# The last four gate groups of a hybrid layer as a seven-product block

## The chip, the cores and the metric

One core of a Trainium2 chip runs the whole layer. The metric is the device time of one execution in microseconds (us). Engines: PE (TensorE, matmul), DVE (VectorE), ACT (ScalarE), POOL (GpSimd), SP (SyncE, which issues most DMA transfers from a queue worked off in order). ACT issues a few transfers from its own queue.

## The reference, cut to what matters

```python
h = rms_norm(x, norm_mix_g)
y_m, y_d, y_c = ...            # mLSTM, differential attention, memory cross-attention
g_m, g_d, g_c = jnp.split(jax.nn.sigmoid(h @ w_gate + b_gate), 3, axis=-1)
merged = g_m * (y_m @ w_proj_m) + g_d * (y_d @ w_proj_d) + g_c * (y_c @ w_proj_c)
x = x + merged @ w_out
h2 = rms_norm(x, norm_mlp_g)
x = x + jnp.square(jax.nn.relu(h2 @ w_up)) @ w_down
```

There are 1024 positions and 1024 channels; `w_gate` is 1024 x 3072. Everything is float32.

## The kernel before

**Products.** A float32 product is made of three matmuls in the `fp32r` type: each operand is split into a high part (a cast on ACT) and a low part (a subtraction on DVE), by `split` (L106), and `mm3` (L117) issues high x high, high x low, low x high. The normed input stands transposed in SBUF as `hT` (8 row tiles of 128 channels, high and low, 64 KB a partition).

**Gates.** The 3072 gate columns are 12 groups of 256. `gate_steps` (L447) is a generator: a group has four quarters (two halves of 128 columns by two halves of 512 positions), a quarter 8 steps of three matmuls, 96 matmuls of 512 columns in a group. Behind a quarter ACT makes the tanh (L471) and SP stores it to DRAM (`gdr`, L472). `gate_load` (L432) loads and splits the weights of the next group, two 128-row tiles a load. The products go to two PSUM banks in turn (`mm_tile`, L144, `kmm = 2`).

**Order.** Groups 0 and 1 fill the cross-attention, 2 and 3 the mLSTM (`branch_m`). Groups 4 and 5 run by themselves. Then `branch_d` (L966), the differential attention: `d_gemm` (L859) makes q, k, v of one head after the other in steps of three matmuls, and the attention's scores, transposes and value products stand between the steps in an order written out by hand; `fill(n)` takes n steps. It begins with `fill(60)` (L1083). After each four row tiles `prep` (L865) turns q and k: a transpose on PE (`pr`), behind a power on POOL (`rsqrt_mean`, L124) and a scaling of k on DVE (`s_`, L884). Behind the last head, groups 6 to 8 are the steps. Groups 9 to 11 run by themselves after the attention. The instructions that are not pinned are placed by the framework's scheduler, on SP too, where a transfer waits in its turn.

**Buffers.** Pools are stacked: each starts at the byte of a partition where the one before it ends, and space of a closed pool is taken over by the next. `hT` lies at 3,072 to 68,608, the split weights (`wpg`, 13 tiles of 3 KB) and the raw weights (`rpg`, 3 of 3 KB) behind it to 117,760. From there come the attention's pools, or, after it, the two gate tiles. A tile of the new owner waits until the old ones at its bytes are read.

**Tail.** `tail` (L1297) starts when `hT` is closed, at byte 3,072. It multiplies the three branches' outputs (`yd` in DRAM) by their projections, first the cross-attention's. `k_tiles` (L1263) loads eight tiles of 128 x 1024 into two buffers (`yrp`, 4 KB each) and splits them into nine places of 8 KB (`ys8` first). `load_w` (L130) loads the weights into two buffers (`rp2`, 4 KB each), 512 KB for four row tiles. Its first group (`group`, L1274, `outer`) goes row tile by row tile through four banks, 12 matmuls for each. The pools ahead of `yrp` are `tone` 4,608 bytes, `ssq` 4 KB, `gl` 4 KB, `mtp` 32 KB, `mlp` 32 KB, `op` 8 KB, `hole` 7 KB and the nine `ys` of 8 KB.

**Seven products.** The MLP (`wino`, L1174) and its second half multiply 256 x 256 blocks of weights by blocks of two row tiles and two halves of the positions with seven products instead of eight. `PROD` (L1121) lists, for each, the weight block and the operand block; the blocks beyond the four plain ones are sums, made by `wino_s` on POOL (L1142) for the weights and `wino_t` on DVE and POOL (L1123) for the operand.

Of the kernel before, what the change touches and what calls it, by code (L numbers as in the profile page):

```python
# [71 lines left out]
class Layer:  # L72
# [359 lines left out]
    def gate_load(self, pool=None):  # L432

        pool = pool or self.gwp
        n = self.gate_n
        if n == 12 * NK:
            return
        g, k = divmod(n, NK)
        if k % 2 == 0:
            self.graw = self.grp.tile([P, 512], F32, tag="raw", name=self.name("raw"))  # L440
            self.nc.sync.dma_start(self.graw.rearrange("p (k n) -> p k n", k=2), self.a["wgate"][g][:, k : k + 2, :])
        t = pool.tile([P, 2, 256], F32R, tag="w", name=self.name("w"))
        self.split(t[:, 0], t[:, 1], self.graw[:, k % 2 * 256 : k % 2 * 256 + 256])
        self.gw.append((t[:, 0], t[:, 1]))
        self.gate_n = n + 1

    def gate_steps(self, runs):  # L447
# [4 lines left out]
        for run in runs:  # L452
            for r in range(run):
# [3 lines left out]
                for q in range(4):  # L457
# [505 lines left out]
                late.pop(0)[1]()  # L963
            yield True

    def branch_d(self, pool):  # L966
        nc = self.nc
        V = nc.vector
        self.pinned = True
# [5 lines left out]
        def fill(n):  # L975
            for _ in range(n):
                r = next(gemm, None)
                if r is None:
                    next(gates, None)
# [100 lines left out]
                nc.scalar.activation(y, pt, AF.Copy, scale=self.gsub)  # L1080
                self.store_y(1, hh // 2, hh % 2, y)

        fill(60)  # L1083
        for s in range(NS + 4):
            hh, i = divmod(s - 2, 4)
            if s < NS:
# [23 lines left out]
                combine(s)  # L1110
        fill(8)
        norm(15, 2)
        assert self.gdone <= 288
        while self.gdone < 288:
            next(gates)
        self.pinned = False


# [497 lines left out]
    def run(self):  # L1616
        tc, nc = self.tc, self.nc
        with ExitStack() as ctx:
# [19 lines left out]
            self.x1d = dt("x1_d", (8, P, D))  # L1638
            self.h2d = dt("h2_d", (8, P, D))
            self.rd = dt("r_d", (16, P, 7, 512))  # L1640
            with ExitStack() as c1:
                E1 = lambda *x, **k: c1.enter_context(tc.tile_pool(*x, **k))
                self.pmm = E1(name="pmm", bufs=1, space=PSUM)
# [4 lines left out]
                with ExitStack() as c2:  # L1648
# [4 lines left out]
                    with tc.tile_pool(name="ptmp", bufs=1) as tmp0, tc.tile_pool(name="ptmp2", bufs=2) as tmp, tc.tile_pool(name="ptmp8", bufs=8) as tmp8:  # L1653
# [24 lines left out]
                    self.branch_m(T3(), gm, 1, gnext)  # L1678
                with tc.tile_pool(name="wpg", bufs=13, reuse_waits="tile") as self.wp, tc.tile_pool(name="rpg", bufs=3, reuse_waits="tile") as self.rp:
                    self.gwp, self.grp = self.wp, self.rp  # L1680
                    with tc.tile_pool(name="pg", bufs=2) as self.gpool:
                        for _ in range(2 * 32):
                            next(self.gates)
                    cg.close()
                    with tc.tile_pool(name="pd", bufs=2) as pd, tc.tile_pool(name="pd3", bufs=3) as pd3, tc.tile_pool(name="pdm", bufs=1) as pdm, tc.tile_pool(name="pd5", bufs=7) as pd5, tc.tile_pool(name="pdv", bufs=5) as pdv, tc.tile_pool(name="pdv2", bufs=17) as pdv2, tc.tile_pool(name="pd4", bufs=4) as pd4:
                        self.tmask = pdm.tile([P, D], F32, name="tmask")
                        nc.gpsimd.memset(self.tmask, 0.0)
                        nc.gpsimd.affine_select(
                            out=self.tmask[:, D - P : D], in_=self.tmask[:, D - P : D], pattern=[[-1, P]],
                            compare_op=ALU.is_ge, fill=NEG, base=0, channel_multiplier=1,  # L1690
                        )
                        class T4:
                            def tile(_, shape, dt, tag, name):
                                tag = "dscr2" if tag == "gt" else tag
                                p = pd5 if tag == "draw" else pdv if tag == "drr" else pdv2 if tag == "dv" else pd4 if tag in ("dk", "dkl") else pdm if tag == "dpe1" else pd3 if tag in ("daT", "dst") else pdm if tag in ("dscr", "dscr2", "y", "dsg") else pd
                                return p.tile(shape, dt, tag=tag, name=name)
                        self.gpool = T4()
                        self.branch_d(T4())
                    with tc.tile_pool(name="pgh", bufs=2) as self.gpool:
                        for _ in self.gates:  # L1700
                            pass
            self.tail()


# [3 lines left out]
def pack(i):  # L1708
# [3 lines left out]
    def grp(w, cols):  # L1712
        return np.ascontiguousarray(w[:, cols].reshape(-1, P, len(cols)).transpose(1, 0, 2))
# [20 lines left out]
        return q.transpose(3, 2, 1, 0, 4)  # L1734

    wg = i["w_gate"][0]
    w["wgate"] = np.stack([grp(wg, r(256 * g, 256)) for g in range(12)])
# [33 lines left out]
```

## Time and profile before

| | |
|---|---|
| median of 3 runs (lowest, highest) | 2207.4 us (2206.66, 2209.99) |
| the profiled execution | 2207.4 us, of it span 2205.3 us |
| PE busy | 2162.5 us, 98% |
| DVE, ACT, POOL busy | 62%, 45%, 24% |
| matmuls of the gates (512 columns) | 1152 |

The span is the time from the first to the last instruction in the trace. Busy times of a group are unions, since matmuls overlap: their mean length is more than the distance at which they follow each other. "L91" is the matmul call that all products share, so products are told apart by their tiles: `mm<-hT,w` are products with `hT` as the moving operand (gates, mLSTM), `mm<-w,hT` the attention's rows, `sc` scores, `po` values, `tp` and `pr` transposes, `mm<-kt,w` the tail's first projection.

### The profile page before, as it was taken

How to read it: one execution, taken by the hardware profiler on the slowest of the kernel's cores; microseconds unless marked ns; L12 is line 12 of the kernel's file. 1: busy time of each engine (PE TensorE's matmuls, PEld its weight loads, DVE VectorE, ACT ScalarE, POOL GpSimd, SP SyncE). 2: the span in 40 equal slices, each digit the busy share in tenths (PEclk: the TensorE clock that was granted, in tenths of full speed). 3: DMA queues.
4: the chain of work that ended last, by engine and by line, in shares of the span. 5: the costliest groups of instructions: out<-in, count | busy, mean ns of one | idle time of the engine just before them, and what ended most of it. 6: DMA issues, size and time to landing. Idle time of an engine off the chain costs nothing.

```text
span 2205.3 us, 30616 instructions
## 1 busy us (share of the span) xinstructions
PE 2162.5 (98%) x11097; PEld 1862.0 (84%) x11097; DVE 1360.7 (62%) x2598; ACT 982.2 (45%) x1962; POOL 525.2 (24%) x696
## 2 busy tenths in 40 slices
PE   7999999999999999999999999999999999999999
PEld 5878888898899999999888888887787888788887
DVE  6643565565237777777641242544588877767779
ACT  6543354454336666666542120314444444543332
POOL 2100000000011111111000002102657655555553
PEclk9999999999999999999999999999999999999999
DMA  7123122121333333333343443436435444854444
GB/s 250 31 78 117 52 92 73 43 81 44 108 109 91 89 87 88 89 90 82 101 153 114 133 161 107 144 103 207 157 106 197 158 150 146 321 195 154 145 140 167
DMA packets 127948, 273.06 MB, mean 124 GB/s; under 512 B 12945, under 2 KB 21430, under 8 KB 125750
## 3 DMA queue, kind: packets, MB, share of 16 engines
q1 hardware_dynamic: 125494, 258.53, 37.2%
q10 hardware_dynamic: 2304, 12.58, 1.4%
q8 instruction: 87, 1.43, 0.3%
q14 instruction: 63, 0.52, 0.1%
HBM read 178.76 MB, written 67.14 MB: 112 GB/s over the span
## 4 chain that ended last, share of the span: by engine, by line
PE 86%; DVE 5%; DMA 4%; ACT 2%; issue 2%; POOL 1%; SPq 0%; DVEq 0%; ACTq 0%; POOLq 0%
PE mm L91 51%; PE p L91 22%; PE sc L91 6%; PE po L91 3%; PE tp L94 3%; DVE acc L67 1%; PE pr L94 1%; DVE wo L67 1%; DVE u L67 0%; DVE w L112 0%; DMA kraw<-y 0%; PE tp L91 0%; DMA wraw<-in_wdown 0%; DVE xts L67 0%; DMA xr<-h_d 0%
## 5 line engine op out<-in xcount | busy, mean ns | idle before, releaser
L91 PE MATMUL mm<-w,hT 128*128 128x384 f32 (+3 forms) x2496 | 471.7, 331 | 2.5 <-ACT w L111 2.4
L91 PE MATMUL mm<-hT,w 128*128 128x512 f32 x1920 | 465.6, 395 | 0.0
L91 PEld LDWEIGHTS mm<-hT,w 128*128 128x128 f32 x1920 | 353.6, 188 | 74.0
L91 PEld LDWEIGHTS mm<-w,hT 128*128 128x128 f32 x2496 | 389.0, 189 | 13.8 <-ACT w L111 3.2
L91 PE MATMUL p<-xo,wo 128*128 128x512 f32 x1344 | 311.0, 393 | 6.4 <-DVE st L1418 3.2
L91 PE MATMUL p<-xd,wo 128*128 128x512 f32 x1344 | 309.5, 392 | 5.5 <-DVE c L67 2.2
L91 PEld LDWEIGHTS p<-xo,wo 128*128 128x128 f32 x1344 | 253.0, 189 | 63.1 <-DVE u L67 3.7
L91 PEld LDWEIGHTS p<-xd,wo 128*128 128x128 f32 x1344 | 253.4, 189 | 61.4 <-DVE c L67 3.3
L91 PE MATMUL mm<-kt,w 128*128 128x512 f32 x1152 | 261.9, 389 | 0.9 <-DVE w L112 0.5
L112 DVE TENSOR_TENSOR w<-raw,w 128x256 fp32r<-128x256 f32 (+3 forms) x304 | 172.8, 588 | 138.2 <-ACT w L111 137.1
L91 PEld LDWEIGHTS mm<-kt,w 128*128 128x128 f32 x1152 | 216.1, 188 | 46.6 <-DVE w L112 1.0
L111 ACT CAST w<-raw 128x256 fp32r<-128x256 f32 (+3 forms) x304 | 154.4, 530 | 176.6 <-PE mm L91 132.1
L104 ACT CAST wo<-wraw 128x896 fp32r<-128x896 f32 x122 | 115.0, 944 | 213.6 <-PE p L91 101.7
L67 DVE TENSOR_TENSOR wo<-wraw,wo 128x896 fp32r<-128x896 f32 x122 | 143.3, 1192 | 58.5 <-ACT wo L104 58.5
L1145 POOL TENSOR_TENSOR wraw<-wraw 128x128 f32<-128x128 f32 x128 | 93.7, 732 | 253.1 <-DMA wraw<-in_wdown 122.9
L1007 ACT ACTIVATE dpe<-sc,dst,drr 128x256 f32<-128x256 f32 (+7 forms) x128 | 106.7, 833 | 95.5 <-DVE dst L1003 92.1
L999 DVE CUSTOM_DVE_ANT_0 sc<-sc,tmask 128x256 f32<-128x256 f32 (+7 forms) x128 | 97.0, 757 | 14.7 <-PE sc L91 14.1
L127 POOL TENSOR_SCALAR hss<-hss 128x4 f32<-128x4 f32 x8 | 3.3, 408 | 415.1 <-ACT mscr L752 273.0
L91 PE MATMUL sc<-dk,dq 128*128 128x512 f32 (+3 forms) x384 | 91.7, 347 | 0.0
L1148 POOL TENSOR_TENSOR wraw<-wraw 128x128 f32<-128x128 f32 x128 | 87.2, 681 | 9.9
L1146 POOL TENSOR_TENSOR wraw<-wraw 128x128 f32<-128x128 f32 x128 | 87.7, 685 | 0.0
L1147 POOL TENSOR_TENSOR wraw<-wraw 128x128 f32<-128x128 f32 x128 | 85.2, 665 | 0.0
(283 smaller groups left out, 2830.7 us busy)
## 6 DMA issues: line engine op xcount, KB each, us to landing
dk<-dsg SPq DMA_DIRECT2D x64, 256.0 KB, 4.2
wraw<-in_wup SPq DMA_DIRECT2D x64, 256.0 KB, 3.4
r_d<-xts SPq DMA_DIRECT2D x16, 1024.0 KB, 4.1
wraw<-in_wdown SPq DMA_DIRECT2D x64, 256.0 KB, 3.1
xd<-r_d SPq DMA_DIRECT2D x19, 768.0 KB, 7.3
xd<-r_d SPq DMA_DIRECT2D x14, 1024.0 KB, 6.7
raw<-in_wgate SPq DMA_DIRECT2D x48, 256.0 KB, 2.9
gates<-gt SPq DMA_DIRECT2D x48, 256.0 KB, 2.0
```

The costliest lines, as they stand in the source:

```text
L67: return self.tc.keep_in_program_order(f(*a, **k))
L91: self.pin(self.nc.tensor.matmul(out, l, r, start=start, stop=stop))
L94: self.pin(self.nc.tensor.transpose(out, x, self.ident))
L104: self.A.copy(hi, src)
L111: nc.scalar.copy(hi, src)
L112: nc.vector.tensor_sub(lo, src, f32(hi))
L999: V.tensor_tensor_reduce(out=sc[:, 0:n], in0=sc[:, 0:n], in1=self.tmask[:, D - n : D], scale=1.0, scalar=-3.0e38, op0=ALU.add, op1=ALU.max ...
L1007: nc.scalar.activation(pe[c][:, 0:n], sc[:, 0:n], AF.Exp, bias=t8[:, 2 + c : 3 + c], scale=rr[:, i, c : c + 1], accum_out=t8[:, 4 + c : 5 ...
L1145: G.tensor_add(r[:, 4], r[:, 0], r[:, 3])
L1146: G.tensor_sub(r[:, 5], r[:, 4], r[:, 1])
L1147: G.tensor_sub(r[:, 6], r[:, 1], r[:, 0])
L1148: G.tensor_sub(r[:, 7], r[:, 2], r[:, 5])
```

## The change

- Gates are direct for groups 0 to 7 only: 0 to 3 as before, group 4 by itself, 5 to 7 in the attention. The stores of groups 5 to 7 are issued by ACT.
- Groups 8 to 11 become `wino_gates`, after the attention: four runs of seven products, each four pairs of row tiles deep, in the two PSUM banks. The three plain operand blocks come from `hT`; the four summed ones (X4, X5, X6, X3; 2 MB each, 16 KB a partition) are loaded from DRAM (`hcd`). The weights come in quads; POOL makes four sums of 256 columns for each of eight loads, and 56 tiles of 256 columns are split.
- `h_sums` makes the four summed blocks and stores them: per pair of row tiles two additions, three subtractions on DVE and one on POOL, then four splits and stores of 512 KB. It advances at every third step of group 4 and at every fourth of `fill(60)`.
- The pools of the attention are reordered and wait by tile; group 4's tanh goes into one tile instead of two. The pools of `wino_gates` stand from byte 117,760: gate tiles 4 KB, `fev` 16 KB, three raw rings of 8 KB, then X3, X6, X5, X4.

```diff
@@ gate_load
-        if n == 12 * NK:
+        if n == 8 * NK:
@@ gate_steps
-                    nc.sync.dma_start(self.gdr[ft, :, s], t)
+                    (nc.scalar if g > 4 else nc.sync).dma_start(self.gdr[ft, :, s], t)
@@ branch_d
-        fill(60)
+        for n in range(60):
+            fill(1)
+            if n % 4 == 3:
+                next(sums, None)
...
-        assert self.gdone <= 288
-        while self.gdone < 288:
+        assert self.gdone <= 256
+        while self.gdone < 256:
             next(gates)
+    def h_sums(self, pool):
+        nc, V, G = self.nc, self.nc.vector, self.nc.gpsimd
+        for kp in range(4):
+            b = []
+            for k in range(2):
+                t = pool.tile([P, D], F32, tag="dpe0", name=self.name("hb"))
+                V.tensor_add(t, f32(self.hT[:, 2 * kp + k, 0]), f32(self.hT[:, 2 * kp + k, 1]))
+                b += [t[:, 0:512], t[:, 512:]]
+                yield
+            V.tensor_sub(b[1], b[0], b[1])
+            G.tensor_sub(b[0], b[2], b[0])
+            V.tensor_sub(b[2], b[2], b[1])
+            yield
+            V.tensor_sub(b[3], b[3], b[2])
+            for i, t in enumerate((b[1], b[2], b[0], b[3])):
+                o = pool.tile([P, 2, 512], F32R, tag="daT", name=self.name("ho"))
+                self.split(o[:, 0], o[:, 1], t)
+                nc.sync.dma_start(self.hcd[i, :, kp], f32(o).rearrange("p a n -> p (a n)"))
+                if i % 2:
+                    yield
+    def wino_gates(self, base):
...
+        gtp, ev, r0, r1, r2 = one("fgt", 2), one("fev", 2), one("fr0"), one("fr1"), one("fr2")
+        x3, x6, x5, x4 = one("fx3"), one("fx6"), one("fx5"), one("fx4")
+        rr = Ring([r2, r1, r0])
...
+        def load(n):
+            if n < 8:
+                u, kk = divmod(n, 2)
+                r = rr.tile([P, 8, 2, P], F32, tag="fr", name=self.name("fr"))
+                for i in range(2):
+                    nc.sync.dma_start(r[:, 0:4, i], self.a["wgq"][u][:, 2 * kk + i])
+                G.tensor_add(r[:, 4], r[:, 0], r[:, 3])
...
+        def wsp():
+            n = len(W)
+            if n < 56:
+                u, r = divmod(n, 14)
+                j, kk = divmod(r, 2)
+                t = self.wp.tile([P, 2, 256], F32R, tag="w", name=self.name("w"))
+                self.split(t[:, 0], t[:, 1], raws[2 * u + kk][:, 1 + self.PROD[j][0]].rearrange("p k n -> p (k n)"))
+                W.append(t)
+                if j == 6:
+                    load(2 * u + 3 + kk)
...
+        for n in range(3):
+            load(n)
+        for q in (4, 5, 6, 3):
+            nc.sync.dma_start(f32(X[q]).rearrange("p k a n -> p k (a n)"), self.hcd[q - 3])
+        for _ in range(9):
+            wsp()
+        self.pinned = True
...
+            for j, (l, q) in enumerate(self.PROD):
+                ps = self.mm_tile()
+                for kp in range(4):
+                    w = W[u * 14 + 2 * j + kp // 2]
+                    c = slice(kp % 2 * P, kp % 2 * P + P)
+                    self.mm3(ps, (w[:, 0, c], w[:, 1, c]), (x_(q, kp, 0), x_(q, kp, 1)), kp == 0, kp == 3)
+                    if kp % 2:
+                        wsp()
...
+                elif j == 5:
+                    V.tensor_add(u3, u3, ps)
+                    V.tensor_add(u2, u2, ps)
+                    out(2, u3)
+                else:
+                    V.tensor_add(u2, u2, ps)
+                    out(0, u2)
@@ run
-                    self.gates = self.gate_steps((2, 1, 1, 2, 6))
+                    self.gates = self.gate_steps((2, 1, 1, 1, 3))
...
+                        sums = self.h_sums(self.gpool)
+                        for n in range(32):
+                            next(self.gates)
+                            if n % 3 == 2:
+                                next(sums)
+                        cg.close()
+                        self.pd4 = E3("pd4", 4)
+                        self.branch_d(T4(), sums)
+                    with ExitStack() as c3:
+                        self.wino_gates(c3)
```

## Rows read from the trace of the kernel before

**Rows 1.** The page, busy us (share of the span) xinstructions
```profile
PE 2162.5 (98%) x11097; PEld 1862.0 (84%) x11097; DVE 1360.7 (62%) x2598; ACT 982.2 (45%) x1962; POOL 525.2 (24%) x696
```

**Rows 2.** Timeline of ACT in the gates (start, us, line, out<-in, idle before)
```profile
603.82 0.69 ACT L471 ACTIVATE gt<-mm,dv 128x512 f32<-128x512 f32 x1 [4.75 <-PE mm L91]
609.25 0.69 ACT L471 ACTIVATE gt<-mm,dv 128x512 f32<-128x512 f32 x1 [4.75 <-PE mm L91]
```

**Rows 3.** Timeline of PE, from the last score to the tail
```profile
1110.05 1.10 PE L91 MATMUL sc<-dk,dq 128*128 128x512 f32 x4
...
1124.96 1.03 PE L91 MATMUL po<-dv,daT 128*128 128x128 f32 x7 [0.33 <-DVE daT L112]
...
1143.93 66.94 PE L91 MATMUL mm<-hT,w 128*128 128x512 f32 x294
1210.71 49.58 PE L91 MATMUL mm<-kt,w 128*128 128x512 f32 x218
```

**Rows 4.** The tail's y tiles: operations (ns min/median/max) and landing
```profile
L111 ACT CAST kt<-kraw x24: 1041/1051/1057, 1153.2 to 1401.4; 128x1024 fp32r<-128x1024 f32 x24
L112 DVE TENSOR_TENSOR kt<-kraw,kt x24: 1211/1224/1433, 1154.2 to 1402.4; 128x1024 fp32r<-128x1024 f32 x24
...
DMA to landing us min/median/max: 3.2/4.2/5.6
```

**Rows 5.** The attention's transposed tiles: splits of up to 512 columns, ns min/median/max
```profile
L111 ACT CAST daT<-tp x96: 253/526/598, 660.6 to 1123.6; 128x512 fp32r<-128x512 f32 x48, 128x128 fp32r<-128x128 f32 x16, 128x256 fp32r<-128x256 f32 x16, 128x384 fp32r<-128x384 f32 x16
L112 DVE TENSOR_TENSOR daT<-tp,daT x96: 279/618/693, 661.2 to 1124.2; 128x512 fp32r<-128x512 f32 x48, 128x128 fp32r<-128x128 f32 x16, 128x256 fp32r<-128x256 f32 x16, 128x384 fp32r<-128x384 f32 x16
```

**Rows 6.** Stretches around the attention's first rows, busy us by engine
```profile
577.00:598.00 21.00, 21.00 (x92) 16.87 (x91) 5.65 (x13) 7.29 (x17) 1.25 (x2) 1.00 0.61 200
...
620.00:640.00 20.00, 20.00 (x119) 19.96 (x118) 4.06 (x12) 5.76 (x17) 1.97 (x2) 1.00 0.20 70
```

**Rows 7.** Timelines of PE, POOL and DVE at the first transposes of k
```profile
619.89 18.91 PE L91 MATMUL mm<-w,hT 128*128 128x384 f32 x108
...
642.74 0.66 PE L94 MATMUL pr<-ident,draw 128*128 128x128 f32 x4
...
638.25 2.91 POOL L128 TENSOR_TENSOR drr<-drr,mhalf 128x16 f32<-128x16 f32 x1
...
641.19 0.90 DVE L887 TENSOR_TENSOR draw<-draw,drr 128x128 f32<-128x128 f32 x4 [0.45 <-POOL drr L128]
```

**Rows 8.** Groups by form (count | busy, mean ns), and ACT's DMA issue
```profile
L112 DVE TENSOR_TENSOR w<-raw,w 128x256 fp32r<-128x256 f32 x14 | 5.4, 421 | 20.2 <-ACT w L111 20.2
...
L111 ACT CAST w<-raw 128x256 fp32r<-128x256 f32 x14 | 5.1, 404 | 7.7 <-DMA raw<-in_wgate 7.2 <-PE mm L91 0.5
...
L1405 ACTq DMA_DIRECT2D r_d<-rq x16: 326/326/342, 1620.3 to 1906.1; - x16
```

**Rows 9.** The page, DMA issues: count, KB each, median us to landing
```profile
xr<-h_d SPq DMA_DIRECT2D x4, 1024.0 KB, 5.3
```

**Rows 10.** PE behind a wait, and two stretches (PEclk is the third number from the end)
```profile
1523.79 0.73 PE L91 MATMUL mm<-mh,w 128*128 128x512 f32 x2 [3.00 <-DVE w L112]
...
1525.00:1528.40 3.40, 3.40 (x9) 2.62 (x9) 1.65 (x2) 0.21 (x1) 0.00 (x0) 0.51 0.76 216
...
1580.00:1587.00 7.00, 6.41 (x16) 5.09 (x17) 5.87 (x10) 5.69 (x9) 6.31 (x9) 0.54 0.29 81
```

**Rows 11.** The MLP: operand subtraction, POOL sums, and a stretch of it
```profile
L1129 DVE TENSOR_TENSOR xts<-xr,xts x4: 678/1667/1671, 1514.7 to 1585.5; 128x512 f32<-128x512 f32 x4
...
L1146 POOL TENSOR_TENSOR wraw<-wraw 128x128 f32<-128x128 f32 x54 | 38.8, 719 | 0.0
...
L1128 POOL TENSOR_TENSOR xts<-rq 128x512 f32<-128x512 f32 x14 | 24.4, 1743 | 5.5 <-DMA r_d<-xts 5.1 <-ACT rq L1404 0.5
...
1680.00:1760.00 80.00, 79.57 (x351) 65.81 (x351) 68.64 (x80) 37.42 (x58) 54.70 (x75) 1.00 0.42 148
```

**Rows 12.** Timeline of SP's queue ahead of the attention
```profile
583.80 2.85 SPq L903 DMA_DIRECT2D raw<-in_wd  x3
```

More of the change, by code (lines that the diff above doesn't have):

```diff
@@ L964, in d_gemm, with branch_d @@
             yield True
-    def branch_d(self, pool):
+    def branch_d(self, pool, sums):
         nc = self.nc
@@ new lines, in wino_gates, with x_, out @@
+    def wino_gates(self, base):
+        nc, V, A, G = self.nc, self.nc.vector, self.nc.scalar, self.nc.gpsimd
+        one = lambda name, bufs=1: base.enter_context(tc.tile_pool(name=name, bufs=bufs, reuse_waits="tile"))
+        tc = self.tc
+        gtp, ev, r0, r1, r2 = one("fgt", 2), one("fev", 2), one("fr0"), one("fr1"), one("fr2")
+        x3, x6, x5, x4 = one("fx3"), one("fx6"), one("fx5"), one("fx4")
+        rr = Ring([r2, r1, r0])
+        X = {}
+        for q, p in ((4, x4), (5, x5), (6, x6), (3, x3)):
+            X[q] = p.tile([P, 4, 2, 512], F32R, tag="x", name=self.name("hx"))
+        raws, W = {}, []
+        def load(n):
[5 more added lines that the diff above has]
+                G.tensor_add(r[:, 4], r[:, 0], r[:, 3])
+                G.tensor_sub(r[:, 5], r[:, 4], r[:, 1])
+                G.tensor_sub(r[:, 6], r[:, 1], r[:, 0])
+                G.tensor_sub(r[:, 7], r[:, 2], r[:, 5])
+                raws[n] = r
+        def wsp():
[8 more added lines that the diff above has]
+                    load(2 * u + 3 + kk)
+        def x_(q, kp, i):
+            if q >= 3:
+                return X[q][:, kp, i]
+            k, hf = divmod(q + 1, 2)
+            return self.hT[:, 2 * kp + k, i, hf * 512 : hf * 512 + 512]
+        for n in range(3):
[5 more added lines that the diff above has]
+        self.pinned = True
+        tl = lambda n: ev.tile([P, 512], F32, tag=n, name=self.name(n))
+        for u in range(4):
+            def out(i, c):
+                ft, s = 16 + u * 2 + i // 2, slice(i % 2 * 512, i % 2 * 512 + 512)
+                t = gtp.tile([P, 512], F32, tag="gt", name=self.name("gt"))
+                A.activation(t, c, AF.Tanh, bias=self.bg[:, ft : ft + 1], scale=0.5)
+                nc.scalar.dma_start(self.gdr[ft, :, s], t)
+            for j, (l, q) in enumerate(self.PROD):
[6 more added lines that the diff above has]
+                        wsp()
+                if j == 0:
+                    u2, c11, u3, c21 = (tl(n) for n in ("u2", "c11", "u3", "c21"))
+                    A.copy(u2, ps)
+                elif j == 1:
+                    V.tensor_add(c11, u2, ps)
+                    out(1, c11)
+                elif j == 2:
+                    V.tensor_add(u2, u2, ps)
+                elif j == 3:
+                    V.tensor_add(u3, u2, ps)
+                elif j == 4:
+                    V.tensor_add(c21, u3, ps)
+                    out(3, c21)
+                elif j == 5:
[3 more added lines that the diff above has]
+                else:
+                    V.tensor_add(u2, u2, ps)
+                    out(0, u2)
@@ L1680, in run @@
                     self.gwp, self.grp = self.wp, self.rp
[L1681 to L1685, printed above, removed]
+                    with ExitStack() as c3:
+                        E3 = lambda name, bufs: c3.enter_context(tc.tile_pool(name=name, bufs=bufs, reuse_waits="tile"))
+                        pdo, pdy, pdv2, pdm, pds, pd5 = E3("pdo", 2), E3("pdy", 1), E3("pdv2", 17), E3("pdm", 1), E3("pds", 1), E3("pd5", 7)
+                        pdv, pd, pd3 = E3("pdv", 5), E3("pd", 2), E3("pd3", 3)
                         self.tmask = pdm.tile([P, D], F32, name="tmask")
@@ L1694, in tile @@
                                 tag = "dscr2" if tag == "gt" else tag
[L1695 removed]
+                                p = {
+                                    "draw": pd5, "drr": pdv, "dv": pdv2, "dk": self.pd4, "dpe1": pdm, "daT": pd3, "dst": pd3,
+                                    "dscr": pds, "dsg": pds, "dscr2": pdy, "y": pdy, "doS": pdo, "dso": pdo,
+                                }.get(tag, pd)
                                 return p.tile(shape, dt, tag=tag, name=name)
                         self.gpool = T4()
[L1698 to L1701, printed above, removed]
+                        sums = self.h_sums(self.gpool)
[6 more added lines that the diff above has]
+                        self.branch_d(T4(), sums)
+                    with ExitStack() as c3:
+                        self.wino_gates(c3)
             self.tail()
@@ L1736, in pack @@
     wg = i["w_gate"][0]
-    w["wgate"] = np.stack([grp(wg, r(256 * g, 256)) for g in range(12)])
+    w["wgate"] = np.stack([grp(wg, r(256 * g, 256)) for g in range(8)])
+    w["wgq"] = quads(wg[:, 2048:])
     for n, s in (("wpm", "w_proj_m"), ("wpd", "w_proj_d"), ("wpc", "w_proj_c"), ("wout", "w_out")):
```

3 lines of the change are left out of this document (added).

## The prediction

> **What bounds the kernel now.** I read the page's busy shares first: TensorE is busy in 98% of the span [rows 1]. So time is saved by fewer matmuls, and lost wherever PE waits; work on DVE, ACT, POOL or a queue costs only where PE comes to wait for it. Then I read the timelines of the stages that change. In the gate groups a TANH starts every 5.44 us [rows 2]; it follows a quarter of a group, 24 matmuls of 512 columns, so a matmul takes 5.44 / 24 = 0.2268 us and PE does nothing else there. Behind the attention PE goes from gates to the first tail product without a gap, at 1210.71 [rows 3]. The last three groups (12 x 5.44 = 65.3 us) thus began at 1145.4. The attention's last score ends near 1112 and its last value product at 1125.8 [rows 3]; what follows until 1145.4 is gates.
>
> **What is removed.** Four groups of 96 matmuls become four of 7 products x 4 pairs x 3 = 84. That is 48 matmuls fewer, 48 x 0.2268 = **10.9 us** less on PE, with no assumption: no wait lies in the old groups to hide in. A group takes 84 x 0.2268 = 19.05 us, a product 2.72 us. That one of the groups moves from ahead of the attention to behind it changes nothing in the sum.
>
> **Operand sums ahead of the attention.** DVE: 8 additions of 1024 columns at 1.22 us, a two-input operation of that width [rows 4], 12 subtractions of 512 and 16 split halves at 0.69 [rows 5], 9.8 + 8.3 + 11.0 = 29.1 us. ACT: 16 casts at 0.59 = 9.4 us [rows 5]. POOL: 4 at 1.74 = 7 us [rows 11]. SP: 16 stores of 512 KB. The portions fall into 21.8 us of the one group left there and 40 row steps of three matmuls (18.91 us for 108 [rows 7], so 0.52 us a step), together 42.6 us, where DVE was busy 5.65 of 21 us and 4.06 of 20 us [rows 6]. It fits, and PE needs none of it before the seven-product block. The cover is thin at one place: the first turning of k. There POOL's power ran from 638.25 to 641.16, DVE's scaling to 642.1, and the transpose stood at 642.74 [rows 7], a slack of 0.65 us. A sum in progress on DVE (1.22) or POOL (1.74) would delay it: at most 1.22 + 1.74 - 0.65 = 2.3 us, once; nothing if the sums are done by then. I take **0.5 us**. A store that waits for its split holds SP's queue for the attention's first weights too, but they have 20 us of group in which to come.
>
> **Inside the block.** 56 weight splits instead of 32, at 0.40 on ACT and 0.42 on DVE [rows 8]; per group ACT has 14 x 0.40 + a copy of 0.6 + 4 tanh of 0.69 [rows 2] + 4 issues of 0.33 = 10.3 us, DVE 14 x 0.42 + 7 additions of 512 columns at 0.69 [rows 5] = 10.7 us, POOL 8 sums. All lie beside 19.05 us of PE. 28 gate stores move from SP's queue to ACT's, 0.33 us each [rows 8]. With two banks a product must be read out within 2.72 us of its end; the sixth has two additions (1.4 us) behind up to two splits (0.84). That holds by 0.5 us when nothing else delays it. From 0 to 0.6 us a group, **0.5 us** taken for all four.
>
> **Into the block.** X4 and X5 lie where the attention's last k tiles were, free after the last score, 33 us before the block. X6 and X3 lie over attention tiles, free after the last value product, 20 us before. A 1 MB load took 5.3 us [rows 9]; 2 MB are at most twice that, 10.6. Two before the values' end, two after it: 21.2 us, against X6 due 20 + 10.9 and X3 due 20 + 13.6 us after the values. Nothing on the path, if SP takes them in that order.
>
> **Out of the block.** This is the largest cost. Adding up the pools (all stacked from the same byte 117,760), X3 takes bytes 162,816 to 179,200 of each partition. The tail, which starts from byte 3,072, puts its y buffers (yrp) at 170,496 to 178,688 and its raw weights (rp2) from 178,688 on. Both overlap X3, and X3 is read until the sixth product of the last group. Before, these loads were done under three groups of gates. Now they can start 2.72 us before the block's end T. With issues of some 0.35 us the first y tile is issued at T - 2.4 and the first weights, third in line, at T - 1.7. By the median of 4.2 us [rows 4] they land at T + 1.8 and T + 2.5. ACT casts y0, y1 and w0, 1.05 us each [rows 4]: w0 is cast at T + 5.0, and PE starts there instead of at T. The low half of w0 comes behind those of y0 and y1 on DVE (1.22 each), at T + 6.5, while PE has only two matmuls (0.45 us) to do: 1.05 us more. So PE idles 6.05 us. The later y tiles come in pairs every 4.2 + 1.05 + 1.22 = 6.5 us or so, against 5.4 us of matmuls for two, but the late start leaves them room.
>
> The clock goes on top. After the 3.0 us wait at 1520.8 the granted clock was 0.51 for 3.4 us; in a second stretch of the MLP's beginning it was 0.54 over 7 us [rows 10]; these are the 1.2 GHz level against 2.4. That costs 1.7 or 3.4 us; I take 1.7, since the first gap is like this one (a projection waiting for a split of its weights). Bounds of the whole entry: 3.9 us with every load at the fastest 3.2 us, w0 right behind y0 and no fall of the clock; 10.9 us with every load at the slowest 5.6 us and the longer fall. I take 6.05 + 1.7 = **7.7 us**.
>
> **The sum.** The profiled execution took 2207.4 us (span 2205.3, 2.1 around it), which is also the median of the three runs. 2207.4 - 10.9 + 0.5 + 0.5 + 7.7 = **2205.2 us**. Two tenths of a per cent, about what a measurement of this kernel can tell from no change, are 4.4 us: under 2203.0 is faster, over 2211.8 slower.
>
> **Rivals.**
>
> *The tail is fed in time.* If the y tiles and weights come early after all, only 1 us of small costs is left: 2207.4 - 10.9 + 1.0 = 2197.5. For it: today the splits of the y tiles begin at 1153.2, in the middle of the gates [rows 4], and the loads go as soon as their bytes are free. Against it: the byte ranges. X3 would have to be read early, and its product is the sixth of seven. Chance 0.15. A lucky middle of the forecast (an entry under 5.5 us) also falls below 2203.0.
>
> *The operands queue in order.* If SP holds the four X loads behind the third raw load, whose bytes hold the last v tile and the mask and come free only with the last value product, X4 starts 20 us before the block. At 10.6 us each they land 10.6, 21.2, 31.8 and 42.4 us later; due are 25, 28, 31 and 33.6. X6 is late by 1.3 and X3 by 8.8 in all. Then 2205.2 + 8.8 = 2214.0, slower; it decides from 33.6 / 4 = 8.4 us a load. For it: SP's queue is worked off in order, so an unready transfer holds those behind it. Against: three weight loads of the attention went out at 583.80, in the middle of groups 4 and 5, whose gate stores the code writes earlier [rows 12], so the order follows readiness; and the 5.3 us of a 1 MB load includes a start that doesn't double. Chance 0.08.
>
> *POOL and DVE hold each other up.* In the MLP's operand sums the same DVE subtraction took 0.68 or 1.67 us [rows 11], about a microsecond more where POOL works beside it. The block puts 8 POOL sums of 256 columns beside every 14 DVE splits. A POOL sum of 128 columns takes 0.72, of 512 1.74 us [rows 11]; for 256, nearer to the narrow one, I put 1.1. If each holds DVE for its whole length, DVE needs 10.7 + 8.8 = 19.5 us a group against PE's 19.05: the edge. At 1.3 us it needs 21.1, 2.05 us over, 8.2 us in four groups: 2205.2 - 0.5 + 8.2 = 2212.9, slower. It decides from (19.05 - 10.7) / 8 = 1.04 us a sum. Against it: from 1680 to 1760 DVE was busy 68.6 and POOL 54.7 of 80 us, and PE still 79.6 [rows 11]. The Trainium skill (SBUF — State Buffer, Who interferes with whom) states it as a rule: a DVE instruction with two SBUF inputs and a GpSimd one that reads SBUF exclude each other, and the second waits out the first. By that rule every split in the block is open to it, and so are the sums ahead of the attention, and the time would be that of this rival. The two durations of the MLP's subtraction agree with the rule; PE's share there says that it need not reach PE. Chance 0.08.
>
> **How the numbers follow.** Forecast 0.60, fed in time 0.15, the two slow rivals 0.16, and 0.09 for others (a shift in the order of some queue) of either sign. Faster: 0.15, a quarter of the forecast (0.15), and 0.03: 0.33. Slower: 0.16 and a little of the rest: 0.18. Within: 0.49. Range: the forecast's bounds are 2207.4 - 10.9 + 3.9 = 2200.4 and 2207.4 - 10.9 + 10.9 + 2.3 + 2.4 = 2212.1; 2199.5 to 2212.5 takes these in and leaves out most of the first rival and part of the slow ones, about two in ten. The forecast's own range is 2200.4 to 2212.1.
>
> **What would show it.** Right: four groups of 84 matmuls at 0.2268 us each; the first y load issued just after the sixth product of the last group; a PE wait of 4 to 6 us at the first tail product, put down to w, kt or their loads, and the granted clock near 0.5 behind it. Wrong: y tiles cast before the block's end; PE waits at the third to sixth product of the first group (X late), or every 2.72 us (read-out late); DVE splits of 256 columns near 1.5 us; a gap at the first transposes of k; or an entry that costs the whole 10.9 us.

## The result and the profile after

The changed kernel takes 2215.2 us (median of 10 runs, 2212.8 to 2220.0), the kernel before on the same chip 2209.8 (10 runs, 2206.7 to 2211.3). The ratio is 1.0029, 95% interval 1.0019 to 1.0039 (it weighs all runs; the medians alone give 1.0025): slower, where 2205.2 of 2207.4 (0.9990) was forecast. The profiled execution took 2214.7 us, of it span 2212.9, against a span of 2205.3 before: 7.6 us more in the span.

The page of after, busy us, against [rows 1]:

```profile
PE 2158.4 (98%) x11049; PEld 1856.0 (84%) x11049; DVE 1424.3 (64%) x2686; ACT 1003.6 (45%) x2006; POOL 561.4 (25%) x732
```

The 48 matmuls are gone (11097 to 11049), as promised. So PE waits somewhere, and the question is where. Four instants cut both spans: the attention's first row (the first matmul of q, k and v), its first score, the end of its last value product, the tail's first row.

| stretch, us | before | after | difference |
|---|---|---|---|
| start to first row | 619.9 | 600.1 | -19.8 |
| first row to first score | 32.2 | 40.6 | **+8.4** |
| first score to last value | 473.9 | 475.5 | +1.6 |
| last value to tail's first row | 84.7 | 105.0 | +20.3 |
| tail's first row to the end | 994.6 | 991.6 | -3.0 |

The first and the fourth belong together, since a group moved from one to the other: +0.5, where -10.9 for the matmuls and some 8 for block and tail were expected.

The timeline of PE in after, from the first row (start, us, line, out<-in, count, idle before), against [rows 7]:

```profile
600.13 4.35 PE L91 MATMUL mm<-w,hT 128*128 128x384 f32 x24
605.25 8.60 PE L91 MATMUL mm<-w,hT 128*128 128x384 f32 x48 [0.77 <-ACT gt L471]
614.22 6.54 PE L91 MATMUL mm<-w,hT 128*128 128x384 f32 x36 [0.37 <-DVE dv L112]
622.92 0.66 PE L94 MATMUL pr<-ident,draw 128*128 128x128 f32 x4 [2.17 <-DVE dv L112]
623.33 2.34 PE L91 MATMUL mm<-w,hT 128*128 128x384 f32 x12
628.21 3.22 PE L91 MATMUL mm<-w,hT 128*128 128x384 f32 x9 [2.55 <-DVE dsg L115]
...
640.77 0.34 PE L91 MATMUL sc<-dk,dq 128*128 128x128 f32 x2
```

Before, 108 row matmuls ran there in 18.91 us without a wait [rows 7]. Now there are four waits, 5.86 us in all, and slow rows behind the last. The timeline of DVE in the same stretch says why:

```profile
587.56 2.35 DVE L1128 TENSOR_TENSOR hb<-hT 128x1024 f32<-128x1024 f32 x2
...
602.70 0.69 DVE L1133 TENSOR_TENSOR hb<-hb,hb 128x512 f32<-128x512 f32 x1 [1.18 <-POOL hb L1132]
...
618.21 1.55 DVE L112 TENSOR_TENSOR ho<-hb,ho 128x512 fp32r<-128x512 f32 x1
619.68 0.68 DVE L1133 TENSOR_TENSOR hb<-hb,hb 128x512 f32<-128x512 f32 x1
620.39 0.69 DVE L1135 TENSOR_TENSOR hb<-hb 128x512 f32<-128x512 f32 x1
621.04 1.29 DVE L112 TENSOR_TENSOR ho<-hb,ho 128x512 fp32r<-128x512 f32 x2
622.25 0.41 DVE L953 TENSOR_REDUCE drr<-dscr 128x4 f32<-128x256 f32 x1
622.58 0.28 DVE L112 TENSOR_TENSOR dv<-mm,dv 128x128 fp32r<-128x128 f32 x1
626.00 0.90 DVE L887 TENSOR_TENSOR draw<-draw,drr 128x128 f32<-128x128 f32 x4 [3.13 <-POOL drr L128]
```

The first sum starts at 587.56, nine us into the one group that is left (which began 21.8 us before the first row, at 578.4). From there to 622.9 DVE is busy for 33.8 of 35.3 us. The split of v (`dv<-mm`, 0.28 us) reads a PSUM bank that PE needs next; it stands behind the sums of the next portion and comes at 622.58. The ACT half of that readout waits too: ACT's casts of the sums wait 3.10 us for DVE and stand ahead of the copies of q, k and v. Timelines of ACT and POOL in after:

```profile
620.39 1.14 ACT L111 CAST ho<-hb 128x512 fp32r<-128x512 f32 x2 [3.10 <-DVE hb L1133]
...
617.91 1.30 POOL L1132 TENSOR_TENSOR hb<-hb,hb 128x512 f32<-128x512 f32 x1 [7.46 <-DVE hb L1128]
```

The end of the values, timelines of PE and of DVE in after, against [rows 3]:

```profile
1115.23 1.01 PE L91 MATMUL po<-dv,daT 128*128 128x128 f32 x7 [1.42 <-DVE daT L112]
```

```profile
1111.07 0.69 DVE L112 TENSOR_TENSOR daT<-tp,daT 128x512 fp32r<-128x512 f32 x1 [4.19 <-ACT daT L111]
1111.68 2.90 DVE L112 TENSOR_TENSOR w<-fr,w 128x256 fp32r<-128x256 f32 x4
1114.50 0.68 DVE L112 TENSOR_TENSOR daT<-tp,daT 128x512 fp32r<-128x512 f32 x1
```

Four splits of the block's first weights stand ahead of the probability split that the last values need: 1.42 us of wait, 0.33 before. The tail, timeline of PE and (next fence) of ACT:

```profile
1200.76 11.04 PE L91 MATMUL mm<-hx,w 128*128 128x512 f32 x48
1211.64 2.88 PE L91 MATMUL mm<-hT,w 128*128 128x512 f32 x12
1221.26 4.14 PE L91 MATMUL mm<-kt,w 128*128 128x512 f32 x8 [6.74 <-issue]
```

```profile
1215.29 1.04 ACT L111 CAST kt<-kraw 128x1024 fp32r<-128x1024 f32 x1 [1.99 <-DMA kraw<-y]
1216.24 0.72 ACT L1197 ACTIVATE gt<-u,dv 128x512 f32<-128x512 f32 x1
1216.86 1.03 ACT L111 CAST kt<-kraw 128x1024 fp32r<-128x1024 f32 x1
...
1220.11 1.04 ACT L111 CAST w<-raw 128x1024 fp32r<-128x1024 f32 x1 [2.23 <-DMA raw<-in_wpc]
```

The block ends at T = 1214.4. ACT casts two y tiles and then waits for the first weights, issued at 1212.70, which took 7.4 us to land; their cast starts at T + 5.7, and PE starts 6.74 us late. At the end of the first rows, behind the last values and at the tail the clock is at the 1.2 GHz level (PEclk is the third number from the end; stretches of after):

```profile
628.40:631.60 3.20, 3.20 (x11) 3.10 (x12) 0.28 (x2) 0.00 (x0) 0.00 (x0) 0.50 0.66 169
1116.60:1119.60 3.00, 3.00 (x8) 2.33 (x8) 1.04 (x2) 0.68 (x2) 0.39 (x2) 0.50 1.04 444
1219.10:1225.50 6.40, 4.22 (x9) 2.97 (x10) 3.32 (x4) 3.74 (x4) 0.00 (x0) 0.50 1.04 415
```

Elsewhere the two executions differ by +2.0 us near 204 us and by about -4 in the MLP, in code that is the same in both: single profiles scatter by that much, so a place is judged by its own rows and a total by all runs. (From the tail's first row to the end, nearly the same code in all, the fourteen profiles of this case took 990.9 to 1002.6 us.)

### The profile page after: what moved, and what is told of

It is laid out like the page before. It is cut to its first block, busy times and chain, and to the rows that moved or that the text cites. A ratio compares the mean times of both kernels' runs of the same rounds, so it can differ in the third digit from the quotient of the medians.

```text
span 2212.9 us, 30757 instructions
## 1 busy us (share of the span) xinstructions
PE 2158.4 (98%) x11049; PEld 1856.0 (84%) x11049; DVE 1424.3 (64%) x2686; ACT 1003.6 (45%) x2006; POOL 561.4 (25%) x732
## 4 chain that ended last, share of the span: by engine, by line
PE 84%; DVE 6%; DMA 5%; ACT 2%; issue 2%; POOL 2%; SPq 0%; DVEq 0%; ACTq 0%; POOLq 0%
PE mm L91 49%; PE p L91 23%; PE sc L91 6%; PE po L91 3%; PE tp L94 3%; DVE w L112 1%; DVE acc L67 1%; PE pr L94 1%; DMA raw<-in_wd 1%; DMA x_d<-gl 1%; DVE wo L67 1%; DMA gates<-gt 1%; DVE u L67 0%; PE tp L91 0%; DMA gl<-in_xT 0%
## 5 line engine op out<-in xcount | busy, mean ns | idle before, releaser
L91 PE MATMUL mm<-hT,w 128*128 128x512 f32 x1680 | 413.8, 397 | 0.2 <-ACT gt L471 0.2
L91 PEld LDWEIGHTS mm<-hT,w 128*128 128x128 f32 x1680 | 309.6, 189 | 65.6 <-ACT gt L471 0.6
L112 DVE TENSOR_TENSOR w<-raw,w 128x256 fp32r<-128x256 f32 (+3 forms) x272 | 162.2, 617 | 79.4 <-ACT w L111 78.4
L111 ACT CAST w<-raw 128x256 fp32r<-128x256 f32 (+3 forms) x272 | 142.0, 546 | 153.6 <-PE mm L91 121.7
L1257 POOL TENSOR_TENSOR wraw<-wraw 128x128 f32<-128x128 f32 x128 | 96.3, 753 | 244.6 <-DMA wraw<-in_wdown 121.2
L1259 POOL TENSOR_TENSOR wraw<-wraw 128x128 f32<-128x128 f32 x128 | 91.0, 711 | 0.0
L104 ACT CAST xd<-xd 128x1536 fp32r<-128x1536 f32 (+2 forms) x36 | 55.0, 1531 | 73.1 <-DMA xd<-r_d 73.1
L1260 POOL TENSOR_TENSOR wraw<-wraw 128x128 f32<-128x128 f32 x128 | 84.3, 658 | 10.0
```

The lines of the kernel that those rows point to most:

```text
L91: self.pin(self.nc.tensor.matmul(out, l, r, start=start, stop=stop))
L104: self.A.copy(hi, src)
L111: nc.scalar.copy(hi, src)
L112: nc.vector.tensor_sub(lo, src, f32(hi))
L1257: G.tensor_add(r[:, 4], r[:, 0], r[:, 3])
L1259: G.tensor_sub(r[:, 6], r[:, 1], r[:, 0])
```

## Experiments

Theory: three things stand in the queues ahead of what PE waits for (sums before the first rows, weight splits before the last values, X3's bytes before the tail), and the sums cost most. Times are given as ratios to before on the same chip, over all runs (ratios of the medians differ from them by up to 0.0006); each 95% interval is 0.001 to 0.0015 to each side, 2 to 3 us. By that measure after is at 1.0029.

**Sums left out.** Stores of plain `hT` halves take the place of the sums, so X4, X5, X6 and X3 hold other values; all transfers remain.

```diff
-                V.tensor_add(t, f32(self.hT[:, 2 * kp + k, 0]), f32(self.hT[:, 2 * kp + k, 1]))
...
+                src = self.hT[:, 2 * kp + k, :, hf * 512 : hf * 512 + 512]
+                nc.sync.dma_start(self.hcd[i, :, kp].rearrange("p (a n) -> p a n", a=2), f32(src))
```

> The arithmetic of the operand sums is left out: the same 8.4 MB go to the same place in 16 stores straight from hT (so four of the seven products have other operands). Theory (the sums fill DVE and ACT while the attention's first rows need them): the PE waits of 5.9 us at the first rows and the fall of the clock behind them go, the stretch from the first row to the first score takes 32.2 us again instead of 40.6, and the time is 2215.2 - 8.4 = 2206.8 us, within 1.5. Rival (the 16 stores in SP's queue, or their traffic, hold up the attention's first weights): the waits stay and the time stays at 2215, within 1.5.

Measured 1.0013 (1.0004 to 1.0022). First row to first score: 32.6 us, 8.0 less than after. The timeline of PE there:

```profile
600.17 18.91 PE L91 MATMUL mm<-w,hT 128*128 128x384 f32 x108
618.92 0.60 PE L94 MATMUL pr<-ident,draw 128*128 128x128 f32 x4
```

The arithmetic, not the 16 stores, costs those 8 us. The time gives back only 0.0016, 3.5 us, and not the 8.4 expected. Part of the difference stands in the profile: PE waited 2.1 us for probability splits in the attention (1.4 in after), and 2.00 us behind a tanh in the gate rows ahead of the block (0.16 in after; see below). The rest isn't shown.

**Two groups ahead of the attention**, three in the block: the sums have twice the time.

```diff
-        if n == 8 * NK:
+        if n == 9 * NK:
...
-        for u in range(4):
+        for u in range(3):
```

> Two direct groups stand ahead of the attention, as before the change, and three instead of four in the seven-product block; the sums have 43.5 us of group instead of 21.8. Theory (too little time for the sums): the 5.9 us of waits at the first rows fall below 1 us and 8.4 us come back, less 12 matmuls of 0.2268 us: 2215.2 - 8.4 + 2.7 = 2209.5 us, within 1.5. Rival (not the room but the sums' order or traffic): the waits stay, 2215.2 + 2.7 = 2217.9.

Measured 1.0030 (1.0018 to 1.0043). First row to first score 34.3 us: of the four waits one is left, 1.59 us, and the clock stays at 1.00. But a group less in the block saves 36 matmuls instead of 48, 2.7 us less, and the tail's wait was 7.35 us. More time ahead of the rows helped the rows; the 5.7 us that the total should have gained by it did not come, and these two items don't account for all of that.

**Summed products first in the last group**. X3's product is then the fourth of seven instead of the sixth, and X3 is read out 8.2 us ahead of the block's end instead of 2.7, two products (5.4 us) earlier:

```diff
+        last = tuple(self.PROD[j] for j in (2, 3, 4, 5, 0, 1, 6))
+        prod = lambda u: last if u == 3 else self.PROD
```

> In the last of the four groups the products with the summed operands come first, the three plain ones last, so X3 is read out three products (8.2 us) earlier than before, 10.9 instead of 2.7 us ahead of the end less its own product: 8.2 us ahead. Theory (the tail's first loads wait for X3's bytes): y tiles and weights land and are split 5.4 us earlier, the PE wait of 6.7 us falls to 0.5 to 1.5 us, the clock doesn't fall there (3.4 us): 2215.2 - 5.5 - 3.4 = 2206.3 us, from 2204.5 to 2209. Rival (another pool or queue sets the start of those loads): the wait stays at 6 to 7 us and the time at 2215.

Measured 1.0024 (1.0014 to 1.0033), not separable from after. The first y load did go out at 1203.71, 8.1 us ahead of the block's end (2.6 in after; two products earlier, not three as the expectation counts), but the tail's wait only fell to 4.27 us. The timeline of ACT shows the next thing that is late:

```profile
1209.63 1.05 ACT L111 CAST kt<-kraw 128x1024 fp32r<-128x1024 f32 x1 [0.40 <-ACT gt L1199]
1214.35 0.72 ACT L1199 ACTIVATE gt<-c,dv 128x512 f32<-128x512 f32 x1 [3.67 <-DMA gates<-gt]
1214.98 1.03 ACT L111 CAST w<-raw 128x1024 fp32r<-128x1024 f32 x1
```

The weights' cast now stands behind a tanh that waits for one of two gate buffers to be stored, where in after it waited for the weights themselves.

**The turned q's low half ahead of k's scaling** (`dsg`, L115, ahead of L887 on DVE), for the largest of the four waits: behind it the scaling waits 3.13 us for POOL's power.

```diff
+                    with self.tc.issue_after(low[0].ins):
+                        self.pin(V.tensor_mul(k_, k_, rr[:, i, 2:4].unsqueeze(2).broadcast_to([P, 2, 64])))
```

> On DVE, the low half of the turned q is put ahead of the scaling of k, which waits for POOL's power; nothing else changes. Theory (part of the loss is the order on DVE, not its load): the 2.5 us wait at the first turning goes, and with it the clock's fall of 1.7 us: 2211 to 2213 us. Rival (DVE is simply full): the wait turns up at the next operation and the time stays at 2215, within 1.

Measured 1.0036 (1.0024 to 1.0048). That wait fell from 2.55 to 0.23 us and the stretch from 40.6 to 37.0, but the waits at the values' end (1.98 us) and at the tail (7.46) were larger, and the 2 to 4 us less that were expected did not come. What this row costs in its own stretch is confirmed, a gain in the total is not.

**Sums at the end of the mLSTM**, in weight buffers of that phase; the group and the first rows have none of them.

```diff
+        sums = self.h_sums()
+        for n in range(20):
+            add(486 + 4 * n, next, sums)
```

> The same sums, stores and operands, but made in the last 55 us of the mLSTM (portions of one kp's halves, in weight buffers of that phase, 32 stores of 256 KB instead of 16 of 512 KB), where VectorE is busy 25 to 45 in 100; nothing of them is left between the last group's weights and the first rows. Theory (the sums' arithmetic fills VectorE's queue ahead of the row read-outs): first row to first score 32.2 to 32.8 us as without the sums (after 40.6), TensorE at rate up to the first row, time 1.0005 to 1.0015 of before. Rival (they cost wherever they stand, since GpSimd and VectorE slow each other and PSUM read-outs queue behind them): the stretch from 485 to 584 us grows by 3 to 8 us and the time stays near 1.003.

Measured 1.0039 (1.0026 to 1.0051): the rival's number. First row to first score is 32.2 us, as before, but the first row comes at 607.68 instead of 600.13. Timeline of PE:

```profile
531.05 2.81 PE L91 MATMUL mm<-w,hT 128*128 128x256 f32 x15 [2.33 <-DVE va L112]
...
556.11 1.91 PE L91 MATMUL mm<-hT,w 128*128 128x512 f32 x7 [0.71 <-DVE w L112]
...
562.54 0.97 PE L91 MATMUL mm<-hT,w 128*128 128x512 f32 x3 [1.34 <-ACT w L111]
```

From 514 to 535 us DVE also has the mLSTM's last convolution, and the readouts of `va` queue again; behind that wait the granted clock is 0.50 from 532.0 to 538.8. The later waits are SP's. Its timeline:

```profile
543.36 14.17 SPq L1144 DMA_DIRECT2D hc_d<-ho  x11
557.62 1.85 SPq L441 DMA_DIRECT2D raw<-in_wgate  x3
```

Each store waits at the head of SP's queue for its sum (35 us in all for the casts of the sums on ACT), with the gate weights behind it.

**The block's first splits behind the last values:**

```diff
+        with tc.issue_after(self.turned[0].ins), tc.issue_after(self.turned[1].ins):
             for _ in range(9):
                 wsp()
```

> Only the block's first nine weight splits are queued on ScalarE and VectorE behind the attention's last probability split. Theory (four splits of the block's first weights, 0.72 us each beside GpSimd's sums, stand ahead of the split that the last values wait for): TensorE's wait there goes from 1.42 us to 0.2 to 0.5 us, no half clock behind it (1.7 us), the block's first product not later; in all 1 to 3 us less than after, 1.0016 to 1.0026 of before. Rival (the split is late for its own cast on ScalarE, or the first product's weights now come late): the wait stays above 1 us, or a new one of 1 us or more stands at the first product; time as after, 1.003.

Measured 1.0041 (1.0028 to 1.0055). PE's wait at the last values is 0.34 us and the clock doesn't fall there, as the theory has it; the sums (40.3 us to the first score) and the tail (7.23 us) are as in after. The total shows no gain: its whole interval lies above the 1.0016 to 1.0026 expected. Up to the tail's first row the profile is 2.5 us ahead of after's (1218.75 against 1221.26), from there to the end 3.1 us behind, in code that is the same.

**Tanh in place**, on top of the order:

```diff
-                t = gtp.tile([P, 512], F32, tag="gt", name=self.name("gt"))
+                t = c if u == 3 else gtp.tile([P, 512], F32, tag="gt", name=self.name("gt"))
```

> The last group's summed products first (as in the run before), and its four tanh write in place, so that they wait for no gate store. Theory (with that order the tail's first weight cast was ready to go 5 us before it went, since it stood on ScalarE behind a tanh that waited for a gate store's landing): wait of TensorE at the tail's first row 4.27 us falls to 0.5 to 2 us and the half clock behind it goes or stays at 3.4 us; 2.5 to 5 us less than with the order alone, time 1.0000 to 1.0015 of before. Rival (the first weights land too late themselves, since the 256 KB gate stores, kraw and raw share the transfers): wait stays at 3.5 us or more, time 1.002.

Measured 1.0036 (1.0022 to 1.0050), and the tail's wait is 6.69 us. The tanh no longer waits, but another instruction took its place in ACT's queue, a cast of the third y tile. Timeline of ACT:

```profile
1217.46 0.72 ACT L1199 ACTIVATE u<-u,dv 128x512 f32<-128x512 f32 x1 [0.22 <-DVE hole L1466]
1221.30 1.04 ACT L111 CAST kt<-kraw 128x1024 fp32r<-128x1024 f32 x1 [3.12 <-DMA kraw<-y]
...
1222.25 1.99 ACT L111 CAST w<-raw 128x1024 fp32r<-128x1024 f32 x2
```

This run also had a wait of 2.44 us in the first rows after the values. ACT's timeline in after has the same cause (PE lost only 0.16 us by it there):

```profile
1121.38 0.33 ACTq L472 DMA_DIRECT2D gates<-gt  x1
1130.95 0.69 ACT L471 ACTIVATE gt<-mm,dv 128x512 f32<-128x512 f32 x1 [9.59 <-DMA gates<-gt]
```

In the attention all tanh share one buffer, and the gate store, 2.1 us by the page's median, takes up to 9.5 us under the 8 MB of X loads.

**Four of them together:** sums in the mLSTM, splits behind the values, summed products first, tanh in place.

> All of it: sums in the mLSTM, the block's splits behind the last values, summed products first in the last group, tanh in place. If the losses are the three named and independent: first rows -8, values' end -1.5 to -3, tail -5 to -8 against after's profile, so 0.997 to 0.9995 of before (2200 to 2205.5 us where before is 2206.6). If a loss given back at one place comes again at the next (the transfers or VectorE are the limit behind all three): 1.001 or more.

Measured 1.0046 (1.0031 to 1.0061): no gain at all. First row at 609.06, a PE wait of 1.91 us behind the tanh, one of 6.65 at the tail. The simple theory (undo three losses, get the 10.9 us) falls. What stays is that behind most removed waits the next one stood, at the next instruction of the same in-order queue (the tail) or in a queue that the removal had filled (the mLSTM).

**Each queue cleared.** On top of that: the sums 26 positions later, past the convolution; their POOL subtraction on DVE; each store issued one portion late; two buffers for the tanh in the attention; the tail's first weights cast ahead of its third y tile.

```diff
+            add(512 + 3 * n, next, sums, None)
...
+                    for d, o in late:
+                        nc.sync.dma_start(d, o)
...
+                    tag = "dscr2" if self.odd else tag
...
+                with self.tc.issue_after(self.hi0.ins):
+                    self.split(t[:, 0], t[:, 1], raw)
```

> Each place where the earlier tries lost time is taken out of its queue: the sums start after the mLSTM's last convolution (26 positions later than in the try before, VectorE 25 in 100 busy there), all on VectorE, each store issued one portion behind its sum; the direct gates' tanh has a second buffer in the attention; the tail's first weights are cast on ScalarE ahead of its third row operand; and, as in the try before, the block's splits stand behind the last values and the last group takes the summed products first. Theory (in-order queues filled ahead of what TensorE waits for, not the amount of work): first row at 600 to 602 us, first row to first score 32.2 to 32.8, the last values to the tail's first row 94 to 99 us (after 105.0, with the order alone 102.2), wait at the tail's first row 0 to 3 us; span 2197 to 2202. Rival (each removed wait turns up again at the next step, as in the try before): first row at 604 or later, or a wait of 5 us at the tail; span 2208 or more.

One run: 2200.25 us, span 2198.2, first row at 597.46, 32.2 us to the first score, 99.3 us from the last value to the tail's first row. The theory's numbers came, with the first row 2.5 us earlier than said and the last stretch 0.3 us above its bound. The early first row is luck: two later kernels with the same code up to there had it at 599.47 and 601.46. What each of the five changes gives by itself was not run. The same kernel, timed:

> The combined kernel again, timed against before: by its stages (first row 2.7 us earlier than after's, first rows 8.4 us shorter, the last values to the tail 5.8 us shorter) 0.9960 to 0.9980 of before. Rival (the single look fell on a fast execution): 0.9990 or more.

**0.9980 of before, 0.9970 to 0.9990**: 2201.8 us (12 runs) against 2205.4 (29 runs). It beats both kernels, though at the upper edge of what was expected. Timeline of PE at the first rows and at the tail:

```profile
599.47 18.91 PE L91 MATMUL mm<-w,hT 128*128 128x384 f32 x108
618.21 0.60 PE L94 MATMUL pr<-ident,draw 128*128 128x128 f32 x4
...
1195.69 8.32 PE L91 MATMUL mm<-hT,w 128*128 128x512 f32 x36
1206.52 18.41 PE L91 MATMUL mm<-kt,w 128*128 128x512 f32 x73 [2.52 <-issue]
```

**One part back at a time**, on the same chip. First block end and tail as in after:

```diff
-        last = tuple(self.PROD[j] for j in (2, 3, 4, 5, 0, 1, 6))
...
-                t = c if u == 3 else gtp.tile([P, 512], F32, tag="gt", name=self.name("gt"))
+                t = gtp.tile([P, 512], F32, tag="gt", name=self.name("gt"))
```

> The combined kernel with the block's end and the tail's start as in after (product order, tanh and first weights untouched). Theory: the wait at the tail's first row comes back as 6.5 to 7.5 us with 6.8 us at half clock, against 2.5 us with 3.4: 4 to 8 us more than the combined kernel, 0.9985 to 1.0005 of before. Rival (the tail's loss was hidden by other work): as the combined kernel within 2 us.

0.9999 (0.9990 to 1.0008), 2205.4 us: 3.6 us more than the combined kernel by the medians, 4.2 by the ratios. The wait is back:

```profile
1212.27 13.07 PE L91 MATMUL mm<-kt,w 128*128 128x512 f32 x46 [7.19 <-issue]
```

Then the sums where after has them, and as after has them (in 512 KB stores, one subtraction of each portion on POOL, no store late):

```diff
-            add(512 + 3 * n, next, sums, None)
...
+            if n % 4 == 3:
+                next(sums, None)
```

> The combined kernel with the operand sums back where after has them, between the last group's weights and the first rows. Theory: first row to first score 39.5 to 41 us instead of 32.2, with 3.4 us at half clock in it: 7 to 10 us more than the combined kernel, 1.0000 to 1.0015 of before. Rival (the sums cost what the run without them showed by the medians, 3.5 us): 0.9985 to 0.9995.

1.0008 (0.9999 to 1.0017), 2208.6 us: 6.8 us more than the combined kernel by the medians, 6.2 by the ratios, and 39.8 us from first row to first score. The wait for the split of v is back too, timeline of PE:

```profile
620.32 0.69 PE L94 MATMUL pr<-ident,draw 128*128 128x128 f32 x4 [2.53 <-DVE dv L112]
...
625.61 1.86 PE L91 MATMUL mm<-w,hT 128*128 128x384 f32 x9 [0.98 <-DVE dsg L115]
```

The rival's range (3.5 us for the sums, 0.9985 to 0.9995) lies below the measured interval, though what the sums cost in all is known from these runs only to some 3 us. The two parts, 10.4 us together, make up most of the way from the combined kernel (0.9980) to after (1.0029), 10.8 us; the 0.4 us left for the splits behind the values and the second tanh buffer are less than these runs can tell.

## Why the prediction was wrong

- **What is removed** was right: 48 matmuls. In the block 48 of them take 10.88 us (the next start, 1211.64, less 1200.76), 0.2267 each (0.2268 said).
- **Operand sums ahead of the attention** is the step that failed: 0.5 us taken, 2.3 as the upper bound, **8.4** measured in the profile's stretch, 8.0 there by leaving them out, 6.2 to 6.8 in the time of the combined kernel by putting them back. Its amounts were right (the eight additions took 1.22 us each, as said). Wrong was "PE needs none of it before the seven-product block", and the cover as a sum of idle time over 42.6 us. PE doesn't need the sums, but it needs the row readouts that stand in the same queues. And the sums weren't spread: they began 9 us into the group and kept DVE full into the first rows, where PE needs a bank read out every 24 matmuls, 4.2 us (18.91 x 24 / 108). One place was looked at where the cover is thin, the turning of k; there were four waits. The largest did come from k's scaling, which POOL's late power held up, but through q's low half that stood behind it on DVE.
- **The end of the values** was not in the sum at all: 0.9 us of added wait (1.42 where 0.33 and 0.20 stood before) and 1.7 of clock (3.4 us at half rate). "Into the block" counted what the X loads need and not what the block's own weight splits do to the values still under way. The run with those splits behind the values shows it, and that the wait can be undone; a gain in the total is not shown for it.
- **Inside the block**: 0.5 us taken; about 0.4 measured, in one of the four runs of seven products (48 matmuls from 1162.26 to 1173.56, 11.3 us instead of 10.9). Right. The wait of 0.16 us for the tanh stands ahead of the block and was not in the sum.
- **Out of the block** was right in its mechanism, and its 7.7 us came, in part by luck: 6.05 us of idle taken, 6.74 measured, and the 1152 tail matmuls took 1.0 us longer than before. The first y load went out at T - 2.6 (T - 2.4 predicted). But the first weights took 7.4 us to land where 4.2 was taken, the second wait of 1.05 us (for their low half) didn't come, and the 1.0 us is 4.3 us of work at half rate less 0.95 us of waits that the tail of before had. The remedy takes more than an earlier load: with the load at T - 8.1 the wait was still 4.27, then 6.69, then 2.52 us, according to what stood ahead of the first weights in ACT's queue.
- The rival **the tail is fed in time** didn't come: PE waited there. Nor did **the operands queue in order**: PE never waits for an X. The X transfers showed otherwise, in a gate store held for 9.5 us beside them. **POOL and DVE hold each other up**: in the block splits grew from 0.42 to at most 0.96 us beside POOL's sums, and PE did not wait for them; ahead of the block it counted. A DVE subtraction that takes 0.68 us took 1.55 beside a POOL subtraction of 1.3, and the four weight splits at 1111.68 took 0.72 us each instead of the 0.42 of [rows 8]. The Trainium skill (SBUF — State Buffer, Who interferes with whom) says that a DVE instruction with two SBUF inputs and a GpSimd one that reads SBUF contend for a port that only one of them holds at a time. These durations agree.
- With the measured terms the sum is 2207.4 - 10.9 + 8.4 + 0.9 + 1.7 + 0.2 + 0.4 + 7.7 = 2215.8 (0.2 the tanh ahead of the block, 0.4 in it); the profile shows 2214.7, with the scatter of +2.0 and -4 in it. Of the 1.6 us between first score and last value 0.9 are the wait at the last values; 0.7 are unexplained, and the combined kernel has 1.1 to 1.6 us there without that wait.

## What to carry over

Work off the critical path isn't free when it fills an in-order queue that also reads PSUM: compare, place by place, how soon the next readout is due with the longest run of such work that can stand ahead of it. Idle time added up over a stretch says only that it can fit. A wait that is removed alone often gives place to the next instruction in the same queue, so read the queue again after each step and judge several removals together.

## What the runs showed that was not expected

- A wait of 1.42 us at the values' end was followed by 3.4 us at the 1.2 GHz level, while one of 1.36 us in the same place (with the sums in the mLSTM) was followed by none: the granted clock there stayed at 1.00. Longer waits, too, went by without a fall: 2.00 us ahead of the block with the sums left out, and 2.53 us at the first transposes in the run with the turned q's low half first. Waits of 6.7 to 7.5 us at the tail went with 6.8 or 10.2 us at that level, the first part of it still within the wait, waits of 2.52 us with 3.4.
- A 256 KB gate store landed in 2.0 to 9.5 us within one kernel; the slow one stood beside the X loads, while the DMA engines were busy for 0.75 of the time (1.04 a little earlier, in the stretch at 1116.6).
